# Seven products instead of eight for the gates of two branches, and the first conditioning blocks in half-width loads, in a decoder layer on one core

## The chip, the core and the metric

The kernel runs on one core of a Trainium2 chip. Every time is in microseconds on the device, of one execution; the time of a kernel is the median of its runs. In the profile PE is TensorE (the matmuls), PEld its weight loads, DVE VectorE, ACT ScalarE, POOL GpSimd, SP SyncE; "SPq" marks the instructions that issue transfers.

## The reference, cut to what matters

One layer over 512 prompt tokens and 8 x 4 sample tokens (544 columns), width 1024, in float32. The `gates` are the last 3 x 1024 columns of the combined input projection.

```python
mod = jax.nn.silu(c) @ lp["w_ada"] + lp["b_ada"]
sh1, sc1, g1, sh2, sc2, g2 = [m[:, None, :] for m in jnp.split(mod, 6, axis=-1)]
h = _rmsnorm(x, lp["norm1_g"]) * (1.0 + sc1) + sh1
z = h @ lp["w_in"]
xa, q, k, v, u, gates = jnp.split(z, list(IN_SPLITS), axis=-1)
...
ga, gb, gc = jnp.split(jax.nn.sigmoid(gates), N_BRANCH, axis=-1)
merged = ga * (ya @ lp["w_branch_a"]) + gb * (yb @ lp["w_branch_b"]) + gc * (yc @ lp["w_branch_c"])
x = x + g1 * (merged @ lp["w_out"])
h2 = _rmsnorm(x, lp["norm2_g"]) * (1.0 + sc2) + sh2
a_up, b_up = jnp.split(h2 @ lp["w_ffn_in"], 2, axis=-1)
x = x + g2 * ((jax.nn.silu(a_up) * b_up) @ lp["w_ffn_out"])
```

## The kernel before, in words

Tokens lie along the free dimension: activations are tiles of 128 features x 544 columns, worked in two halves of `H2` = 272. A float32 product is made of three matmuls on a reduced type: each weight tile is split into a rounded part (`whi`, cast on ScalarE) and a rest (`wlo`, VectorE), each activation likewise ("hh" and "hl" for the normed input, 8 tiles each), and a product is hi·hi, lo·hi, hi·lo. So a 128 x 128 weight tile costs 3 matmuls for each half of 272 columns.

All operations are first recorded by the class `Program`, whose `run` puts them in one fixed order per engine with a list scheduler (costs written in the code, priorities by place in the program, `P.high()` puts some first). An engine then works off its order and waits where an operand isn't ready. As one helper issues everything, all rows have line L428; the names of the tiles tell operations apart. Tiles come from pools of fixed size: 56 slots for activations, three raw weight tiles of 1 MiB, four `whi` and four `wlo` tiles of 128 x 512, 4 `aux` and 2 `mm` tiles in PSUM.

The stages in order: (1) the front: x is loaded and turned, the conditioning vector is multiplied with blocks of 512 columns of w_ada (`ada_load`, `ada`: 8 matmuls, a copy to "adae", 4 transposes, a sum on VectorE into "modT"), blocks 2 (scale) and 0 (shift) first, for the first four tiles of the input, blocks 3 and 1 for the other four; `modulate` makes "hf", "hh" and "hl" of a tile. A half block of w_in ("rawx") is loaded for the first main product. (2) The input projection, pooling, attention and the SSM, whose preparation ("vv", "Bb", "Oc") VectorE does beside the products. (3) The three branches: for a pair of output tiles, `gate` multiplies the normed input with the gate's weights (2 x 8 weight tiles, tanh on ScalarE), `mix` multiplies the branch's result with its weights (2 x 4 weight tiles) and merges on VectorE ("tg") and GpSimd; in most pairs a conditioning block is done between. The first branch (b = 0) has its gates computed earlier. (4) w_out, the residual, the second norm, and the FFN, whose `pair` already uses the two-by-two scheme of seven products: sums of weight tiles ("ws") and of activation tiles ("tsum", "th", "tl") on VectorE in place of one product of eight. At the end of the third branch the input is loaded again ("xagain") for the residual.

Of the kernel before, what the change touches and what calls it, by code (L numbers as in the profile page):

```python
# [432 lines left out]
def body(tc, I, O, dbg=None):  # L433
# [4 lines left out]
    with ExitStack() as ctx:  # L438
# [64 lines left out]
        for i, nme in enumerate(("ssm_b_re", "ssm_b_im")):  # L503
            G.dma_start(brow[32 * i:32 * i + 32], I[nme][0].rearrange("g p c -> g (p c)"))
# [10 lines left out]
        up, dp = up, dp  # L515
        ssm = SSM(tc, I, O, locals())
        ssm.load(brow)
# [6 lines left out]

# [51 lines left out]

        def half_u(i, raw):
# [51 lines left out]
        def modulate(k0, scale9, shift9, name):  # L629

            ks = slice(k0, k0 + 4)
            V.tensor_tensor(xs[:, ks], xs[:, ks], scale9[:, ks, 1:9, None].to_broadcast([128, 4, NB, TS]), op=OP.mult)
            V.tensor_tensor(xs[:, ks], xs[:, ks], shift9[:, ks, 1:9, None].to_broadcast([128, 4, NB, TS]), op=OP.add)
            pairs = []
            for k in range(k0, k0 + 4):
# [94 lines left out]
        h1 += modulate(4, sc1, modT[:, 0:8], "h")  # L730
# [355 lines left out]

        yb = [split_a(ybT[t], "yb") for t in range(4)]
        ssm.stage2()
        branch(1, yb, load_b, (4, 5, 8, 9))


# [174 lines left out]
        def product(ps, w, act, start):  # L1266
            for k in range(4):
                (wh, wl), (ah, al) = w[k], act[k]
                with P.unit():
                    for j, (a, b) in enumerate(((wh, ah), (wh, al), (wl, ah))):  # L1270
                        PE.matmul(ps, a, b, start=start and k == 0 and j == 0, stop=k == 3 and j == 2,
                                  skip_group_check=True)

        def pair(i):
# [6 lines left out]
            a0, a1, b0, b1 = a[:, 0:4], a[:, 4:8], b[:, 0:4], b[:, 4:8]  # L1281
            pb, pa_, pd = aux()[:, :H2], mmt()[:, 0, :H2], aux()[:, :H2]
            part, u3, c = st([128, 2, H2], "part"), st([128, 2, H2], "u3"), st([128, N], "ff")
            cl, cr = c[:, t0], c[:, t1]
            product(pb, quarter(a0), X00, True)
            with P.high():
                S.copy(part[:, 0], pb)
            product(pa_, quarter(a1), X10, True)
            with P.high():
                V.tensor_tensor(cl, pa_, part[:, 0], op=OP.add)  # L1290
                S.activation(cl, cl, AF.Silu)
            s1, s2, s3, s4 = (P.tile(up, [128, 4, 128], F32, "ws", "ux", 4) for _ in range(4))
            with P.high():
                V.tensor_tensor(s1, b0, b1, op=OP.add)
                V.tensor_tensor(s2, s1, a0, op=OP.subtract)
            product(pb, quarter(s2), T2, False)
            with P.high():
                S.copy(part[:, 1], pb)
            product(pd, quarter(s1), T1, True)
            with P.high():  # L1300
                V.tensor_tensor(s3, a0, b0, op=OP.subtract)
            product(pb, quarter(s3), T3, False)
            with P.high():
                S.copy(u3[:, 0], pb)
                V.tensor_tensor(u3[:, 0], pd, u3[:, 0], op=OP.add)
            product(pb, quarter(b1), T4, False)
            with P.high():
                V.tensor_tensor(s4, a1, s2, op=OP.subtract)
            product(pd, quarter(s4), X11, False)
            with P.high():  # L1310
                V.tensor_tensor(cr, pd, part[:, 1], op=OP.add)
                V.tensor_tensor(cl, cl, pb, op=OP.mult)
                S.activation(cr, cr, AF.Silu)
            V.tensor_tensor(cr, cr, u3[:, 0], op=OP.mult)
# [4 lines left out]


        t0, t1 = slice(0, H2), slice(H2, N)
        room = P.tile(up, [128, 7, N], F32R, "tsum", "T", 1)
        homes = [room[:, i] for i in range(7)]

        def home(name):
            return homes.pop() if homes else st([128, N], name, F32R)

        T13, T42 = [], []
        for k in range(4):
          with P.high():  # L1330
            ga, gb = gfs[k], gfs[k + 4]
# [472 lines left out]
```

## Time and profile before

| | |
|---|---|
| median of 3 runs | 924.0 us (922.94 to 925.2) |
| the profiled execution: its own time | 922.1 us |
| its span | 920.3 us |
| TensorE busy | 877.9 us, 95% |
| VectorE, ScalarE, GpSimd busy | 571.3, 409.3, 105.4 us |

Durations of matmuls overlap, since they are pipelined: what one costs is read from the distance of starts in an unbroken stretch. A row of the timeline with "x4" stands for 4 in a row of one kind, with the start of the first and the length of all. In a row of the chain likewise. "[1.49 <-ACT hh L428]" is idle time ahead of the instruction and what ended it.

### The profile page before, as it was taken

The numbers are of one execution on the slowest core, as the hardware profiler recorded it, in microseconds if no ns is written. First come the engines' busy times: TensorE is split into PE (matmuls) and PEld (weight loads), VectorE is DVE, ScalarE is ACT, GpSimd is POOL, SyncE is SP. The second block draws the span as 40 slices with busy tenths as digits, with TensorE's granted clock in tenths as the row PEclk, the third lists the DMA queues.
The fourth block names the chain that finished last, engine by engine and source line by source line (L and its number), as shares of the span: only waits on it lengthen the run. The fifth ranks groups of instructions, "written<-read, shape, count | busy, mean of one in ns | idle before, by whom it ended". The sixth has DMA issues, their size and how long they took to land.

```text
span 920.3 us, 17574 instructions
## 1 busy us (share of the span) xinstructions
PE 877.9 (95%) x7064; PEld 822.7 (89%) x7064; DVE 571.3 (62%) x1230; ACT 409.3 (44%) x871; POOL 105.4 (11%) x128
## 2 busy tenths in 40 slices
PE   3899999999989999999999989999999999999996
PEld 1399988998869999999999789999999999999996
DVE  5776778654845223533336798874588874588743
ACT  6464433355553222423344545552255552255554
POOL 4001000254720111012112000000000000000020
PEclk9999999999999999999999999999999999999998
DMA  9863423410214665255524533223433223432212
GB/s 294 317 204 85 120 75 84 136 47 24 80 24 129 186 183 171 93 186 180 185 71 130 167 94 92 69 70 92 138 92 92 71 73 92 134 93 64 68 54 97
DMA packets 128078, 107.14 MB, mean 116 GB/s; under 512 B 4058, under 2 KB 110942, under 8 KB 127973
## 3 DMA queue, kind: packets, MB, share of 16 engines
q1 hardware_dynamic: 127357, 105.24, 37.8%
q8 instruction: 55, 0.90, 0.4%
q0 software_dynamic: 544, 0.75, 0.3%
q14 instruction: 26, 0.21, 0.1%
q10 hardware_dynamic: 96, 0.04, 0.0%
HBM read 102.39 MB, written 4.81 MB: 116 GB/s over the span
## 4 chain that ended last, share of the span: by engine, by line
PE 80%; DVE 11%; DMA 3%; ACT 3%; issue 1%; SPq 1%; POOL 0%; DVEq 0%; ACTq 0%
PE mm L428 55%; PE aux L428 26%; DVE wlo L428 3%; DMA rawx<-in_w_in_dram 2%; ACT whi L428 1%; DVE ffl L428 1%; DVE gf L428 1%; DVE Hst L428 1%; DMA xtok<-in_x_prompt_dram 1%; DMA raw<-in_w_ffn_in_dram 1%; DVE vv L428 1%; SPq L428 1%; DVE rm L428 1%; DVE rn L428 0%; DVE sc L428 0%
## 5 line engine op out<-in xcount | busy, mean ns | idle before, releaser
L428 ACT CAST whi<-raw 128x512 fp32r<-128x512 f32 x224 | 137.3, 614 | 242.4 <-PE mm L428 195.1
L428 DVE TENSOR_TENSOR wlo<-raw,whi 128x512 fp32r<-128x512 f32 x224 | 159.3, 713 | 109.4 <-ACT whi L428 108.3
L428 PE MATMUL mm<-hh,whi 128*128 128x272 f32 x608 | 133.7, 301 | 1.5 <-ACT hh L428 1.5
L428 PE MATMUL mm<-hl,whi 128*128 128x272 f32 x608 | 125.8, 288 | 0.4 <-DVE hl L428 0.4
L428 PE MATMUL mm<-hh,wlo 128*128 128x272 f32 x608 | 125.6, 288 | 0.0
L428 PEld LDWEIGHTS mm<-hh,whi 128*128 128x128 f32 x608 | 94.5, 189 | 13.5 <-issue 9.3
L428 PEld LDWEIGHTS mm<-hl,whi 128*128 128x128 f32 x608 | 95.3, 188 | 0.6 <-DVE hl L428 0.6
L428 PEld LDWEIGHTS mm<-hh,wlo 128*128 128x128 f32 x608 | 95.4, 188 | 0.0
L428 ACT CAST whi<-ws 128x512 fp32r<-128x512 f32 x80 | 48.8, 619 | 66.7 <-PE aux L428 51.3
L428 PE MATMUL mm<-ffh,whi 128*128 128x272 f32 x328 | 68.3, 289 | 0.0
L428 PE MATMUL mm<-ffl,whi 128*128 128x272 f32 x328 | 67.8, 288 | 0.0
L428 PE MATMUL mm<-ffh,wlo 128*128 128x272 f32 x328 | 67.8, 288 | 0.0
L428 POOL TENSOR_TENSOR ssq<-ssq,sq 128x544 f32<-128x544 f32 x10 | 13.6, 1361 | 423.2 <-ACT sq L428 423.2
L428 DVE TENSOR_TENSOR wlo<-ws,whi 128x512 fp32r<-128x512 f32 x80 | 54.4, 688 | 8.8 <-ACT whi L428 5.9
L428 DVE SCALAR_TENSOR_TENSOR xback<-mm,modT,xback 128x272 f32<-128x272 f32 (+3 forms) x64 | 28.4, 479 | 50.0 <-PE mm L428 50.0
L428 PE MATMUL aux<-tsum,whi 128*128 128x272 f32 x280 | 59.2, 291 | 0.0
L428 PE MATMUL aux<-tl,whi 128*128 128x272 f32 x200 | 57.7, 288 | 0.0
L428 PE MATMUL aux<-ghi,wlo 128*128 128x272 f32 x160 | 47.5, 297 | 5.0 <-DVE wlo L428 4.8
L428 PEld LDWEIGHTS mm<-ffh,wlo 128*128 128x128 f32 x328 | 51.5, 188 | 0.0
L428 PEld LDWEIGHTS mm<-ffl,whi 128*128 128x128 f32 x328 | 51.5, 188 | 0.0
L428 PEld LDWEIGHTS mm<-ffh,whi 128*128 128x128 f32 x328 | 51.4, 188 | 0.0
L428 PE MATMUL aux<-th,wlo 128*128 128x272 f32 x160 | 46.2, 289 | 0.0
(414 smaller groups left out, 2067.9 us busy)
## 6 DMA issues: line engine op xcount, KB each, us to landing
raw<-in_w_ada_dram SPq DMA_DIRECT2D x23, 1024.0 KB, 6.5
raw<-in_w_ffn_in_dram SPq DMA_DIRECT2D x44, 512.0 KB, 5.2
raw<-in_w_in_dram SPq DMA_DIRECT2D x16, 1024.0 KB, 6.4
raw<-in_w_ffn_out_dram SPq DMA_DIRECT2D x16, 512.0 KB, 3.8
raw<-in_w_out_dram SPq DMA_DIRECT2D x4, 1024.0 KB, 5.6
raw<-in_w_ffn_out_dram SPq DMA_DIRECT2D x8, 384.0 KB, 3.4
xtok<-in_x_prompt_dram SPq DMA_DIRECT2D x8, 256.0 KB, 6.2
T<-gd SPq DMA_DIRECT2D x32, 64.0 KB, 3.0
```

The source lines that it names most:

```text
L428: return p.add(tag, cost, lambda: fn(*a, **k), ins, writes, fset, nbytes, after, lock)
```

## The change

Two edits. The gates of branches two and three (b = 1, 2) are computed by `seven`, which is taken out of the FFN's `pair` and serves both, except for the first pair of branch two (b = 1, m2 = 0), which keeps the plain gates. With a0, a1 the two halves of the first output tile's weights along the input and b0, b1 those of the second, seven products of 4 tiles each give both output tiles; `sums` makes the sums of the normed input once ("xsum", then "th" and "tl" as `XH`), and each pair makes four sums of weights. In the plain pair the two gates were followed by their mixes in turn; now the two gates come first and then both mixes (the scheduler decides the order).

The second edit: blocks 2 and 0 are loaded and done in halves of 256 columns (`ada_half_load`, `ada_half`), whose rows in memory are 1 KB long; the half block of w_in is loaded third, and `modulate` is called for two, two and four tiles. With it two loads of ssm_b move from GpSimd's queue to ScalarE's, and the small vectors' loads move ahead of those of the SSM.

```diff
-            G.dma_start(brow[32 * i:32 * i + 32], I[nme][0].rearrange("g p c -> g (p c)"))
+            S.dma_start(brow[32 * i:32 * i + 32], I[nme][0].rearrange("g p c -> g (p c)"))
...
+        def ada_half_load(blk, h, home):
+            SY.dma_start(home.rearrange("p (k n) -> p k n", k=KT),
+                         I["w_ada"][0, :, 512 * blk + 256 * h:512 * blk + 256 * h + 256].rearrange("(k p) n -> p k n", p=128))
+            return home
+
+        def ada_half(blk, h, raw):
+
+            ps = aux()[:, 0:256]
+            mm = []
+            for k in range(KT):
+                g = k % 4
+                mm.append(PE.matmul(ps[32 * g:32 * g + 32], cT[:, k, :], raw[:, 256 * k:256 * k + 256],
+                          start=k < 4, stop=k >= 4, tile_position=(0, 32 * g)))
+            ev = st([128, 256], "adah")
+            S.copy(ev, ps)
...
-        first = ada_load(2)
-        second = ada_load(0, (raw_tile(), big[:, 0:2048]))
+        first = [(b, 0, ada_half_load(b, 0, raw_tile())) for b in (2, 0)]
         rawA = half_u(0, big[:, 2048:4096])
+        second = [(2, 1, ada_half_load(2, 1, raw_tile())), (0, 1, ada_half_load(0, 1, big[:, 0:2048]))]
...
-        ada(2, first)
-        early = [ada(0, second)]
+        for x in first:
+            early = [ada_half(*x)]
+        h1 = modulate(0, 2, sc1, modT[:, 0:8], "h")
+        for x in second:
+            ada_half(*x)
         third, fourth = ada_load(3), ada_load(1)
         ssm.load2(early)
-        h1 = modulate(0, sc1, modT[:, 0:8], "h")
+        h1 += modulate(2, 2, sc1, modT[:, 0:8], "h")
...
-                for m in (2 * m2, 2 * m2 + 1):
-                    tg = gate(b, m, rg)
-                    if m == 2 * m2 and m2 < len(blks):
-                        ada(blks[m2])
-                    mix(b, m, rb, y, tg)
+                if b == 1 and m2 == 0:
+                    tg, u3 = gate(b, 0, rg), gate(b, 1, rg)
+                else:
+                    tg, pb, u3 = seven(rg[:, 0:4, 0:128], rg[:, 4:8, 0:128], rg[:, 0:4, 128:256], rg[:, 4:8, 128:256], XH,
+                                       AF.Tanh, 0.5, "tg")
+                    with P.high():
+                        S.activation(u3[:, t0], pb, AF.Tanh, scale=0.5)
+                        S.activation(u3[:, t1], u3[:, t1], AF.Tanh, scale=0.5)
+                if m2 < len(blks):
+                    ada(blks[m2])
+                mix(b, 2 * m2, rb, y, tg)
+                mix(b, 2 * m2 + 1, rb, y, u3)
...
+        def sums(full, act):
...
+            for k in range(4):
+              with P.shift(0 if full is None else -10 ** 6):
+                if full is None:
+                    ga, gb = (st([128, N], "xsum") for _ in range(2))
+                    for g, (hi, lo) in ((ga, act[k]), (gb, act[k + 4])):
+                        V.tensor_tensor(g, hi.bitcast(F32), lo.bitcast(F32), op=OP.add)
+                else:
+                    ga, gb = full[k], full[k + 4]
+                V.tensor_tensor(ga[:, t0], ga[:, t1], ga[:, t0], op=OP.subtract)
+                V.tensor_tensor(ga[:, t1], gb[:, t1], ga[:, t1], op=OP.subtract)
+                V.tensor_tensor(gb[:, t1], gb[:, t1], ga[:, t0], op=OP.subtract)
+                V.tensor_tensor(gb[:, t0], gb[:, t0], gb[:, t1], op=OP.subtract)
+                for g, dst in ((ga, T13), (gb, T42)):
+                    hi, lo = home("th"), home("tl")
+                    S.copy(hi, g)
+                    V.tensor_tensor(lo, g, hi.bitcast(F32), op=OP.subtract)
+                    dst.append((hi, lo))
...
+            s1, s2, s3, s4 = (P.tile(up, [128, 4, 128], F32, "ws", "ux", 4) for _ in range(4))
+            with P.high():
+                V.tensor_tensor(s1, b0, b1, op=OP.add)
+                V.tensor_tensor(s2, s1, a0, op=OP.subtract)
+            product(pb, quarter(s2), X["T2"], False)
...
+        XH = sums(None, h1)
         branch(1, yb, load_b, (4, 5, 8, 9))
```

**The first weight loads, on SyncE** ("raw" and "rawx" are weight tiles of 1 MiB, w_ada the conditioning blocks). Before:

```order
L428 DMA raw<-in_w_ada_dram 128x4x512 x3
L428 DMA rawx<-in_w_ada_dram 128x4x512
L428 DMA rawx<-in_w_in_dram 128x4x512
L428 DMA raw<-in_w_ada_dram 128x4x512 x4
L428 DMA raw<-in_w_in_dram 128x4x512
```

With the change:

```order
L428 DMA raw<-in_w_ada_dram 128x8x256 x2
L428 DMA rawx<-in_w_in_dram 128x4x512
L428 DMA raw<-in_w_ada_dram 128x8x256
L428 DMA rawx<-in_w_ada_dram 128x8x256
L428 DMA raw<-in_w_ada_dram 128x4x512 x4
```

The w_in tile moved from fifth to third place, and four loads have 256 columns instead of 512.

**The first "hl" tiles, on VectorE** (the rests of the normed input; "t", "qi", "P", "aden", "Pr", "Bb", "vv" are the SSM's preparation). Before:

```order
L428 TENSOR_TENSOR wlo<-rawx,whi 128x512 x4
L428 TENSOR_TENSOR modT<-modT,vT 128x36
L428 TENSOR_TENSOR vm<-Ps,Bbw 128x512
L428 SCALAR_TENSOR_TENSOR sc_103<-modT,vT 128x36
L428 TENSOR_REDUCE modT<-aux 128x36
L428 TENSOR_TENSOR xs<-xs,sc_103 128x128
L428 TENSOR_TENSOR modT<-modT,vT 128x36
L428 TENSOR_TENSOR vv<-vv,vm 128x512
L428 TENSOR_TENSOR xs<-xs,modT 128x128
L428 TENSOR_SCALAR hf<-aux,sc_103,modT 128x512
L428 TENSOR_TENSOR vv<-Pr,Bb 128x512
L428 TENSOR_TENSOR hl<-hf,hh 128x544 x2
```

With the change, the first two tiles, and some 20 rows further the next two:

```order
L428 TENSOR_TENSOR wlo<-rawx,whi 128x512 x4
L428 TENSOR_TENSOR xs<-xs,modT 128x64
L428 TENSOR_SCALAR hf<-aux,sc_103,modT 128x512
L428 SCALAR_TENSOR_TENSOR ang<-rk,ang 128x320
L428 COPY rho_241<-RHO 64x16
L428 TENSOR_TENSOR hl<-hf,hh 128x544 x2
```

```order
L428 TENSOR_SCALAR hf<-aux,sc_103,modT 128x512
L428 TENSOR_TENSOR aden<-aden,t_223 128x32
L428 TENSOR_TENSOR qi<-qi,t_224 128x32
L428 COPY P_243<-Pi 64x16
L428 RECIPROCAL aden<-aden 128x32
L428 TENSOR_TENSOR hl<-hf,hh 128x544 x2
```

Two tiles now stand ahead of most of the preparation, which stands between them and the next two.

**One pair of the third branch, on VectorE** ("tg" and "u" are the gates, "mgl" the rests of the merged result). Before:

```order
L428 SCALAR_TENSOR_TENSOR tg<-tg,mm 128x544
L428 TENSOR_TENSOR wlo<-raw,whi 128x512
L428 SCALAR_TENSOR_TENSOR mgl<-merged,mgh 128x544
L428 TENSOR_TENSOR wlo<-raw,whi 128x512 x2
L428 SCALAR_TENSOR_TENSOR tg<-tg,mm 128x544
```

With the change:

```order
L428 TENSOR_TENSOR tg<-aux,part 128x272
L428 TENSOR_TENSOR wlo<-raw,whi 128x512
L428 SCALAR_TENSOR_TENSOR tg<-tg,mm 128x544
L428 TENSOR_TENSOR wlo<-ws,whi 128x512
L428 SCALAR_TENSOR_TENSOR u_1080<-u_1080,mm 128x544
L428 TENSOR_TENSOR wlo<-ws,whi 128x512
L428 SCALAR_TENSOR_TENSOR mgl<-merged,mgh 128x544
L428 TENSOR_TENSOR wlo<-ws,whi 128x512
L428 TENSOR_TENSOR tg<-mm,part 128x272
```

Between the merges stand the splits of the weight sums, and the gates' own adds of 272 columns.

## Rows read from the trace of the kernel before

**Rows 1.** The page: busy times, the clock by slices, the chain's shares.

```profile
PE 877.9 (95%) x7064; PEld 822.7 (89%) x7064; DVE 571.3 (62%) x1230; ACT 409.3 (44%) x871; POOL 105.4 (11%) x128
...
PEclk9999999999999999999999999999999999999998
...
PE 80%; DVE 11%; DMA 3%; ACT 3%; issue 1%; SPq 1%; POOL 0%; DVEq 0%; ACTq 0%
PE mm L428 55%; PE aux L428 26%; DVE wlo L428 3%; DMA rawx<-in_w_in_dram 2%; ACT whi L428 1%; DVE ffl L428 1%; DVE gf L428 1%; DVE Hst L428 1%; DMA xtok<-in_x_prompt_dram 1%; DMA raw<-in_w_ffn_in_dram 1%; DVE vv L428 1%; SPq L428 1%; DVE rm L428 1%; DVE rn L428 0%; DVE sc L428 0%
```

**Rows 2.** The chain up to 60 us: start, length, what, how many.

```profile
52.22 7.89 PE mm L428 x63
```

**Rows 3.** Windows: stretch, length, busy time (instructions) of each engine, clock, DMA.

```profile
425.20:443.25 18.05, 18.05 (x147) 18.05 (x146) 6.68 (x10) 5.87 (x11) 3.34 (x2) 1.00 0.37 110
...
571.20:582.30 11.10, 10.79 (x84) 10.57 (x84) 9.54 (x18) 6.50 (x14) 0.00 (x0) 1.00 0.33 92
...
270.00:309.00 39.00, 39.00 (x334) 36.57 (x333) 16.26 (x28) 13.34 (x28) 1.35 (x1) 1.00 0.41 122
...
30.00:40.00 10.00, 6.74 (x50) 4.17 (x49) 10.00 (x21) 7.18 (x16) 0.00 (x0) 1.00 0.64 224
40.00:50.00 10.00, 10.00 (x72) 7.17 (x72) 2.96 (x10) 2.99 (x6) 0.00 (x0) 1.00 0.89 335
```

**Rows 4.** TensorE's waits over the span: total us, times, longest.

```profile
PE aux L428 <- DVE wlo L428: 4.8, 14, 0.5
PE aux L428 <- DVE vv L428: 2.7, 2, 1.3
```

**Rows 5.** The chain up to 60 us, its front part.

```profile
13.69 15.44 DMA rawx<-in_w_in_dram
...
29.80 2.50 DVE wlo L428 x4
```

**Rows 6.** Timeline of TensorE, 35 to 46 us.

```profile
35.54 0.52 PE L428 MATMUL mm<-hh,whi 128*128 128x272 f32 x2 [1.49 <-ACT hh L428]
36.47 0.52 PE L428 MATMUL mm<-hl,whi 128*128 128x272 f32 x2 [0.40 <-DVE hl L428]
...
39.97 1.05 PE L428 MATMUL aux<-raw,cT 128*32 128x512 f32 x2
...
41.53 1.06 PE L428 MATMUL aux<-raw,cT 128*32 128x512 f32 x6
```

**Rows 7.** Timeline of TensorE in one FFN pair.

```profile
571.38 0.40 PE L428 MATMUL aux<-ghi,wlo 128*128 128x272 f32 x1 [0.32 <-DVE wlo L428]
...
582.49 0.39 PE L428 MATMUL aux<-ghi,wlo 128*128 128x272 f32 x1 [0.32 <-DVE wlo L428]
```

**Rows 8.** VectorE's groups, 571.2 to 582.3 us, and (last) 425.2 to 461.3.

```profile
L428 DVE TENSOR_TENSOR wlo<-raw,whi 128x512 fp32r<-128x512 f32 x4 | 2.7, 686 | 0.1
...
L428 DVE TENSOR_TENSOR ffl<-ff,ffh 128x544 fp32r<-128x544 f32 x1 | 0.7, 718 | 0.0
...
L428 DVE TENSOR_TENSOR ff<-aux,part 128x272 f32<-128x272 f32 x1 | 0.4, 436 | 0.0
...
L428 DVE SCALAR_TENSOR_TENSOR tg<-tg,mm 128x544 f32<-128x544 f32 x4 | 2.9, 722 | 7.9 <-PE mm L428 7.9
```

**Rows 9.** Timeline of SyncE, 440 to 470 us.

```profile
451.01 3.43 SPq L428 DMA_DIRECT2D xagain<-in_x_prompt_dram  x7
```

**Rows 10.** Timeline of TensorE, 459 to 468 us.

```profile
461.38 3.45 PE L428 MATMUL aux<-ca,xagain 32*128 32x32 f32 x32
```

**Rows 11.** Transfers, 20 to 27 us (w_ada) and 52 to 54.5 (w_in, 256 columns).

```profile
DMA packets 1355, 2.71 MB, mean 387 GB/s; under 512 B 36, under 2 KB 36, under 8 KB 1354
...
DMA packets 856, 0.87 MB, mean 347 GB/s; under 512 B 8, under 2 KB 856, under 8 KB 856
```

**Rows 12.** Timeline of VectorE, 24 to 42 us.

```profile
29.06 0.68 DVE L428 TENSOR_TENSOR vv<-Pr,Bb 128x512 f32<-128x512 f32 x1
...
38.91 0.73 DVE L428 TENSOR_TENSOR hl<-hf,hh 128x544 fp32r<-128x544 f32 x1
```

More of the change, by code (lines that the diff above doesn't have):

```diff
@@ L523, in body @@
         G.dma_start(vrow[68:76], I["final_norm_g"].rearrange("(a b) -> a b", b=128))
+        up, dp = up, dp
+        ssm = SSM(tc, I, O, locals())
+        ssm.load(brow)
         cT = ct([128, KT, 32], "cT")
@@ L627, in body, with modulate @@
         S.copy(xs, turned_samples())
[L629 to L633, printed above, removed]
+        def modulate(k0, n, scale9, shift9, name):
+            ks = slice(k0, k0 + n)
+            V.tensor_tensor(xs[:, ks], xs[:, ks], scale9[:, ks, 1:9, None].to_broadcast([128, n, NB, TS]), op=OP.mult)
+            V.tensor_tensor(xs[:, ks], xs[:, ks], shift9[:, ks, 1:9, None].to_broadcast([128, n, NB, TS]), op=OP.add)
             pairs = []
-            for k in range(k0, k0 + 4):
+            for k in range(k0, k0 + n):
                 src = turned(k)
@@ new lines, in product, with seven @@
+        def product(ps, w, act, start):
+            for k in range(4):
+                (wh, wl), (ah, al) = w[k], act[k]
+                with P.unit():
+                    for j, (a, b) in enumerate(((wh, ah), (wh, al), (wl, ah))):
+                        PE.matmul(ps, a, b, start=start and k == 0 and j == 0, stop=k == 3 and j == 2,
+                                  skip_group_check=True)
+        def seven(a0, a1, b0, b1, X, func, scale, name):
+            pb, pa_, pd = aux()[:, :H2], mmt()[:, 0, :H2], aux()[:, :H2]
+            part, u3, c = st([128, 2, H2], "part"), st([128, N], "u3"), st([128, N], name)
+            cl, cr, ur = c[:, t0], c[:, t1], u3[:, t1]
+            product(pb, quarter(a0), X["X00"], True)
+            with P.high():
+                S.copy(part[:, 0], pb)
+            product(pa_, quarter(a1), X["X10"], True)
+            with P.high():
+                V.tensor_tensor(cl, pa_, part[:, 0], op=OP.add)
+                S.activation(cl, cl, func, scale=scale)
+            s1, s2, s3, s4 = (P.tile(up, [128, 4, 128], F32, "ws", "ux", 4) for _ in range(4))
+            with P.high():
+                V.tensor_tensor(s1, b0, b1, op=OP.add)
+                V.tensor_tensor(s2, s1, a0, op=OP.subtract)
+            product(pb, quarter(s2), X["T2"], False)
+            with P.high():
+                S.copy(part[:, 1], pb)
+            product(pd, quarter(s1), X["T1"], True)
+            with P.high():
+                V.tensor_tensor(s3, a0, b0, op=OP.subtract)
+            product(pb, quarter(s3), X["T3"], False)
+            with P.high():
+                S.copy(ur, pb)
+                V.tensor_tensor(ur, pd, ur, op=OP.add)
+            product(pb, quarter(b1), X["T4"], False)
+            with P.high():
+                V.tensor_tensor(s4, a1, s2, op=OP.subtract)
+            product(pd, quarter(s4), X["X11"], False)
+            with P.high():
+                V.tensor_tensor(cr, pd, part[:, 1], op=OP.add)
+                S.activation(cr, cr, func, scale=scale)
+            return c, pb, u3
@@ L1264, in plain_pair @@
             return split_a(f, "ff")
[L1266 to L1272, printed above, removed]
         def pair(i):
@@ L1280, in pair @@
                 SY.dma_start(v, w_ff[:, c0:c0 + 128].rearrange("(k p) n -> p k n", p=128))
-            a0, a1, b0, b1 = a[:, 0:4], a[:, 4:8], b[:, 0:4], b[:, 4:8]
-            pb, pa_, pd = aux()[:, :H2], mmt()[:, 0, :H2], aux()[:, :H2]
-            part, u3, c = st([128, 2, H2], "part"), st([128, 2, H2], "u3"), st([128, N], "ff")
+            c, pb, u3 = seven(a[:, 0:4], a[:, 4:8], b[:, 0:4], b[:, 4:8], XG, AF.Silu, 1.0, "ff")
             cl, cr = c[:, t0], c[:, t1]
-            product(pb, quarter(a0), X00, True)
             with P.high():
[L1287 to L1311, printed above, removed]
                 V.tensor_tensor(cl, cl, pb, op=OP.mult)
-                S.activation(cr, cr, AF.Silu)
-            V.tensor_tensor(cr, cr, u3[:, 0], op=OP.mult)
+            V.tensor_tensor(cr, cr, u3[:, t1], op=OP.mult)
             return split_a(c, "ff")
@@ L1318, in body @@
         plain = [plain_pair(i) for i in range(2)]
[L1321 to L1331, printed above, removed]
[L1332 to L1343 removed]
+        XG = sums(gfs, hh)
         for part, FH in enumerate(PARTS):
```

37 lines of the change are left out of this document (21 added, 16 removed).

## The prediction, made before the changed kernel ran

> **What bounds the kernel now.** I read the page first: busy times, the slices, the chain that ended last. TensorE is busy 877.9 of 920.3 us, its granted clock stands at full speed in all slices but the last, and the chain is 80% PE, of which "mm" and "aux" matmuls make 81 points [rows 1]. So a matmul that goes is time that goes, wherever TensorE never waits. The time that each main matmul takes can't be read from its duration (288 ns, since neighbours overlap); it is read from a stretch of the chain: 63 in 7.89 us, 0.1252 us each [rows 2]. The windows say the same of one pair of the third branch: 18.05 us for 144 matmuls, 0.1253 us each, with TensorE busy through the whole of it, VectorE 6.68 us and ScalarE 5.87 [rows 3]. The list of TensorE's waits has none between 287 and 462 us, where branches two and three lie; of the waits behind the front two recur below: for the SSM preparation on VectorE ("vv", 2.7 us) and in the seven-product pairs of the FFN ("wlo", 14 waits, 4.8 us) [rows 4].
>
> At the start it is different. There the chain is a transfer, then VectorE: the first half block of w_in lands at 29.13 us (13.69 + 15.44), ScalarE and VectorE split it, VectorE's four "wlo" end at 32.3, and only then come the operations that end in "hl" [rows 5]. The first main matmul is at 35.54, the first on "hl" at 36.47; from there TensorE has work nearly all the time [rows 6].
>
> **The gates, part by part.** A plain pair of gates is 2 x 8 tiles x 3 products x 2 column halves = 96 matmuls; by seven products it is 7 x 4 x 3 = 84, of the same shape. Seven pairs: 84 fewer, **84 x 0.1253 = 10.5 us**, if TensorE stays fed. The same rewrite exists already in the FFN, so its price is on the trace: one pair takes 11.10 us for 84 matmuls (10.53 by the pace), VectorE busy 9.54 us of it, so 0.57 us are lost [rows 3], in a "wlo" that is late for the second product or the last one [rows 7]. Will the branches lose as much? Their pair carries 48 mix matmuls besides, so it lasts (84 + 48) x 0.1253 = 16.5 us. VectorE has in it 9 "wlo" and 4 weight sums of 0.69, three adds of 0.44, two "tg" of 0.72, and in branch three two "mgl" as long as a "tg" [rows 8]: 13 x 0.69 + 3 x 0.44 + 2 x 0.72 = 11.7, 13.2 with the last. That is 71 to 80% against 86% in the FFN pair, and the order puts most mix matmuls between the sum products, where the FFN pair starves. I take 0.15 us for each pair, **1.0 us** in all; ends nothing and 7 x 0.57 = 4.0 us.
>
> [...]
>
> The activation sums XH are new: eight adds of 544 columns, sixteen differences of 272, eight "tl" of 544, or 16 x 0.72 + 16 x 0.44 = 18.6 us of VectorE, and eight casts on ScalarE. They stand in VectorE's order from about 269 us (time of before) and are first read after the first plain pair's gates, one conditioning block and the mixes, about 309 us. In 270 to 309 VectorE is busy 16.26 of 39.00 us [rows 3]: 22.7 are free, so they fit; each may hold a "wlo" up by its own 0.72 us, and a "wlo" ready before it is needed absorbs that. Cost **0**; if the cover were gone, up to 18.6.
>
> At the end of branch three SyncE issues two loads of w_out and then seven of the input for the residual; the last of these are read right after the branch. Before, they were issued from 451.01 to 454.4, and TensorE turned to them at 461.38 [rows 9, 10]. A pair shorter by 1.5 us, and raw tiles that come free later within it, cut this margin of 7 us; I take **0.5 us**, ends 0 and 1.
>
> **The front.** Blocks 2 and 0 come in halves of 256 columns, and the w_in half block goes third of five instead of fifth. The five loads of 1 MiB end with it at 29.13 before. Their rows in HBM shrink from 2 KB to 1 KB; loads of such rows elsewhere move 347 GB/s against 387 [rows 11], so 1.05 MB takes 3.02 us instead of 2.71, 1.2 us more over four. The last load then lands at 30.3, the fourth at 27.3, w_in at 24.3, **4.8 us earlier**. Whi to wlo as before ends about 27.4, "hf" and "hl" follow, and the first "hl" matmul can start near 29.5 instead of 36.47.
>
> [...]
>
> But not 7 us are won. Half a block makes two of the four first "hl"; the others wait for the last half (30.3), its matmuls, its copy and transpose, its "modT" rows, two "hf", and the SSM preparation that VectorE's and ScalarE's orders now hold between. Laid end to end with the durations of before, they come at 38.5 to 39.4; before, the last was 38.91 to 39.6 [rows 12]. So what TensorE wins is what it may do between 29.5 and 39.3 with two of the tiles: 30 main matmuls and all of block 3. Before it had done that by about 45, but with 2.5 us of block 1 in between, which is still to do after: 24 main matmuls ahead, 24 x 0.1252 = 3.0 us, and the wait for "adae" inside 39.97 to 41.5, about 1 us [rows 6], which a matmul now fills. **Gain 4.0**; lowest 2, if the first tiles come two or three us late, highest 7, if nothing holds the second half up.
>
> Moved onto this ground: VectorE's SSM preparation ends later (its "vv" began at 29.06) [rows 12]. Between 40 and 50 VectorE was busy 2.96 of 10 us [rows 3], which takes in that work; what does not fit shows at the "vv" waits. The ssm_b loads go from POOL's queue to ScalarE's and vrow's transpose to before 20 us: neither ends a chain, 0.
>
> **Sum.** The profiled execution took 922.1 us, 1.8 more than its span of 920.3 (the same afterwards, I take it). 922.1 - 10.5 + 1.0 + 0.5 - 4.0 = 909.1. The median of the runs is 1.9 above that execution, so **911.0**. Bounds: 84 matmuls with no stall, front 7: 924.0 - 10.5 - 7 = 906.5; stalls 4.0, residual 1, front 2: 924.0 - 10.5 + 5.0 - 2 = 916.5. Change within 0.2% (1.85 us) can't be told from none here.
>
> **Rivals.** *B, the front gives nothing.* The last "hl" is as late as before, and VectorE's postponed preparation runs into the "vv" waits, which are VectorE's already. For it: VectorE is full from 30 to 40 (10.00) [rows 3]. Against: 7 us free in the next ten. 911.0 + 4.0 = **915.0**. *C, the pairs lose as in the FFN*, 0.57 each: for it, 13 operations of 0.69 in a row when weights of a pair land together; against, the mixes that fill. 911.0 + 3.0 = **914.0**; with B 918.0. *D, slower than before*: the sums XH, issued into one in-order VectorE queue ahead of "wlo" that TensorE reads, are exposed. All of it gives 911.0 + 18.6 = **929.6**; it decides from 13 us exposed, 70% of it. Against: 22.7 us free there, and whi and wlo have four buffers each. *E, the change doesn't do what it says*: pairs last as long as before because something other than the count of matmuls sets them, 911.0 + 9.5 = **920.5**, or no change at all with B, 924.5. Against: TensorE has no idle in a pair, and the weight loads fall with the matmuls.
>
> **Chances.** Forecast 0.62 (own range 906.5 to 913.5), B 0.20, C 0.11 with or without B, D 0.04, E 0.03. From 905 to 918 takes in all of the first three but tails, and leaves some 0.15 out. Faster by over 0.2%: the first three and the half of E that ends at 920.5, 0.94; same 0.02; slower D, 0.04.
>
> **What would show it.** In the profile after: mm and aux matmuls of 272 columns 84 fewer; a pair of branch three 16.5 to 16.7 us long, with TensorE's idle under 0.2 in each; no wait for "xsum", "tl" or "wlo" between 265 and 310; w_in landing near 24.3 and the last half at 30.3; the first main matmul near 28.5 and the last of the first four "hl" at 38.5 to 39.5; TensorE at 60 us some 4 us ahead in matmuls done. It is wrong if TensorE waits over 0.5 us in each pair, if "vv" waits grow by more than 2 us, or if the first "hl" matmul is after 33.

## The result, and the profile after

The changed kernel takes 913.2 us (median of 4 runs, 912.69 to 914.04) against 924.1 before (4 runs): ratio 0.9882, interval 0.9867 to 0.9897, or 10.9 us less, where the sum of the forecast had 13.1. A later set of 5 runs gave 913.98 and 0.9902 (0.9884 to 0.9920).

The page answers to [rows 1] with busy times and the chain's shares:

```profile
PE 870.1 (95%) x7012; PEld 815.3 (89%) x7012; DVE 633.4 (69%) x1339; ACT 435.4 (48%) x936; POOL 107.3 (12%) x126
...
PE 81%; DVE 10%; DMA 4%; ACT 3%; issue 1%; SPq 0%; DVEq 0%; ACTq 0%
```

VectorE has 62 us more to do, TensorE 8 us less, and TensorE is as much the chain as before. The trace has 5676 matmuls of 272 columns where before has 5760: the 84. Two pairs of the third branch in the windows (columns as in [rows 3]); the first has an idle of 0.2 us ahead of a product, the other none:

```profile
415.06:432.09 17.03, 16.85 (x135) 16.64 (x133) 13.95 (x23) 8.95 (x19) 3.35 (x2) 1.00 0.29 94
432.09:448.63 16.54, 16.54 (x134) 16.48 (x132) 10.90 (x16) 8.91 (x19) 3.54 (x2) 1.00 0.65 213
```

The plain pair took 18.05. To see where the rest went I cut each span at three events that all kernels have: the last merge of the first branch on VectorE, the first transpose of the input read back on TensorE, and the first reciprocal of the second norm on VectorE. The differences between them, in us, for this kernel and those of the experiments (one profiled execution each):

| kernel | up to the last merge | branches two and three | read-back, w_out | rest |
|---|---|---|---|---|
| before | 288.2 | 173.2 | 49.5 | 409.4 |
| changed | 285.4 | 163.3 | 53.1 | 410.4 |
| changed, again | 286.0 | 163.1 | 52.8 | 410.3 |
| gates only | 290.2 | 165.6 | 51.5 | 408.8 |
| halves only | 286.1 | 173.2 | 49.4 | 409.2 |
| read-back first | 285.4 | 165.7 | 49.7 | 410.3 |
| read-back first, again | 285.1 | 166.4 | 49.7 | 410.0 |
| first tiles ahead | 286.0 | 166.3 | 51.4 | 410.9 |
| second half on VectorE | 284.8 | 163.0 | 51.4 | 410.8 |
| combo | 285.7 | 163.0 | 49.6 | 410.8 |
| combo, again | 283.9 | 163.0 | 49.6 | 409.5 |
| filler | 284.7 | 162.8 | 49.6 | 412.2 |
| sums more | 285.6 | 165.0 | 51.1 | 409.9 |
| eight pairs | 293.6 | 169.0 | 51.2 | 410.4 |

So from before to changed: the front won 2.8, the branches 9.9, the read-back lost 3.6 of it, and the rest 1.1 (by unrounded times), which makes the 8.0 us between the two spans. (The medians are 10.9 apart, because before's profiled execution, 922.1 us, was faster than the four that give its median, and the changed kernel's, 914.0, the slowest of its four.)

TensorE's waits show the read-back as a new line; the others have changed little against [rows 4]:

```profile
PE aux L428 <- DVE wlo L428: 4.9, 14, 0.5
...
PE mm L428 <- ACT hh L428: 2.5, 1, 2.5
PE aux L428 <- DVE vv L428: 2.3, 3, 1.4
PE aux L428 <- POOL sc L428: 2.3, 3, 1.8
...
PE aux L428 <- DMA xagain<-in_x_prompt_dram: 1.7, 2, 1.4
```

And three windows of 4 us, with the granted clock (the share of its full speed that TensorE was given) as the third column from the end. It is at 1.00 nearly everywhere, but not in the first and the last of these:

```profile
32.00:36.00 4.00, 4.00 (x28) 2.64 (x27) 1.88 (x11) 3.91 (x8) 0.00 (x0) 0.57 1.04 382
256.00:260.00 4.00, 3.62 (x26) 2.12 (x24) 2.17 (x7) 3.45 (x13) 2.82 (x3) 1.00 0.00 0
452.00:456.00 4.00, 3.66 (x21) 3.52 (x19) 0.86 (x2) 2.59 (x5) 0.00 (x0) 0.57 0.71 243
```

0.57 over 4 us is a stretch mostly at 0.50, the granted clock from 32.5 to 35.5 us and from 452.5 to 455.5: 0.43 x 4 = 1.7 us of matmul work lost in each, an estimate from the granted share. Ahead of the first TensorE had waited 2.5 us for the first tile of the normed input, ahead of the last 1.4 us for the read-back. Before's profiled execution had its clock at 1.00 in both places, from 28 to 44 us and from 448 to 464. Its mean granted clock, 0.997, is at the top of what 38 later runs of before show, 0.992 to 0.997; the nine runs of the changed kernel show 0.991 to 0.993.

The read-back on TensorE, which answers to [rows 10], and what SyncE issued, to [rows 9]:

```profile
448.72 1.04 PE L428 MATMUL aux<-ca,xagain 32*128 32x32 f32 x10
451.16 0.98 PE L428 MATMUL aux<-ca,xagain 128*128 128x128 f32 x7 [1.40 <-DMA xagain<-in_x_prompt_dram]
452.49 1.75 PE L428 MATMUL aux<-ca,xagain 128*128 128x128 f32 x7 [0.34 <-DMA xagain<-in_x_prompt_dram]
```

```profile
424.16 13.40 SPq L428 DMA_DIRECT2D raw<-in_w_out_dram  x2
437.62 1.03 SPq L428 DMA_DIRECT2D xagain<-in_x_sample_dram  x2
438.69 1.37 SPq L428 DMA_DIRECT2D xagain<-in_x_prompt_dram  x3
441.13 0.38 SPq L428 DMA_DIRECT2D raw<-in_w_out_dram  x1
441.61 3.07 SPq L428 DMA_DIRECT2D xagain<-in_x_prompt_dram  x5
```

The second load of w_out stands in the queue until a raw tile is free (13.40 us for two issues, 12.6 of them a wait for VectorE's "wlo"), and a third comes between the loads of the input; the last of them are issued up to 444.7 and TensorE turns to them at 448.7: 4 us, where before had 7. The load of w_out between them, issued at 441.13, lands at 449.8, 1 us after TensorE has turned to the input.

### The profile page after: what moved, and what is told of

Read it like the earlier page. It is cut to its first block, busy times and chain, and to the rows that moved or that the text cites. A ratio compares the mean times of both kernels' runs of the same rounds, so it can differ in the third digit from the quotient of the medians.

```text
span 912.3 us, 17678 instructions
## 1 busy us (share of the span) xinstructions
PE 870.1 (95%) x7012; PEld 815.3 (89%) x7012; DVE 633.4 (69%) x1339; ACT 435.4 (48%) x936; POOL 107.3 (12%) x126
## 4 chain that ended last, share of the span: by engine, by line
PE 81%; DVE 10%; DMA 4%; ACT 3%; issue 1%; SPq 0%; DVEq 0%; ACTq 0%
PE mm L428 47%; PE aux L428 34%; DVE wlo L428 3%; ACT whi L428 2%; DVE ffl L428 1%; DMA raw<-in_w_ada_dram 1%; DVE gf L428 1%; DMA xagain<-in_x_prompt_dram 1%; DMA raw<-in_w_ffn_in_dram 1%; DMA xtok<-in_x_prompt_dram 1%; DVE Hst L428 1%; DVE sc L428 0%; DVE vv L428 0%; DVE rm L428 0%; DVE ws L428 0%
## 5 line engine op out<-in xcount | busy, mean ns | idle before, releaser
L428 ACT CAST whi<-raw 128x512 fp32r<-128x512 f32 (+1 forms) x217 | 132.4, 614 | 179.4 <-PE mm L428 125.3
L428 DVE TENSOR_TENSOR wlo<-raw,whi 128x512 fp32r<-128x512 f32 (+1 forms) x217 | 152.9, 710 | 71.6 <-ACT whi L428 69.8
L428 PE MATMUL mm<-hh,whi 128*128 128x272 f32 x412 | 95.1, 306 | 2.5 <-ACT hh L428 2.5
L428 PE MATMUL mm<-hl,whi 128*128 128x272 f32 x412 | 87.7, 289 | 0.3 <-DVE hl L428 0.3
L428 PE MATMUL mm<-hh,wlo 128*128 128x272 f32 x412 | 87.7, 289 | 0.0
L428 PEld LDWEIGHTS mm<-hl,whi 128*128 128x128 f32 x412 | 65.8, 189 | 0.6 <-DVE hl L428 0.6
L428 PEld LDWEIGHTS mm<-hh,wlo 128*128 128x128 f32 x412 | 65.6, 189 | 0.0
L428 DVE SCALAR_TENSOR_TENSOR xback<-mm,modT,xback 128x272 f32<-128x272 f32 (+3 forms) x64 | 28.5, 479 | 50.5 <-PE mm L428 50.4
L428 PE MATMUL aux<-tsum,wlo 128*128 128x272 f32 x216 | 62.0, 287 | 0.0
L428 PE MATMUL aux<-th,whi 128*128 128x272 f32 x216 | 62.0, 287 | 0.0
L428 PEld LDWEIGHTS aux<-tsum,whi 128*128 128x128 f32 x378 | 60.7, 188 | 0.9 <-ACT u L428 0.4
```

Source lines behind the costliest of these rows:

```text
L428: return p.add(tag, cost, lambda: fn(*a, **k), ins, writes, fset, nbytes, after, lock)
```

## The experiments

Each was timed in 5 rounds beside the kernel before on the same chip; the ratios are to that kernel.

**Gates only.** The front of before, the gates of the change (the diff is that of the change without its first part).

```diff
+        XH = sums(None, h1)
```

> The gates alone, on the front of before. Theory: 84 matmuls fewer are worth 10.5 us in the branches, TensorE doesn't wait within a pair (0.2 us in all after), and some 3 us go again where the input is read back for the residual (1.7 us of waits and as much by the halved clock behind them): 924.1 - 10.5 + 3.4 = 917.0, ratio 0.992. First rival (the pairs lose 0.57 each as in the FFN): 924.1 - 6.5 + 3.4 = 921. Second rival (the read-back stall belongs to the earlier front and not to the gates): no stall here, 913.6.

917.33 us, ratio 0.9932 (0.9918 to 0.9945): the theory's time, though not by its terms. The branches shortened by 7.6 us in this profile (table). The read-back has 1.3 us of waits, so it belongs to the gates, but no fall of the clock behind them (1.00 from 448 to 460): its stretch is 2.0 us longer than before's, not 3.4. The 7.6 instead of 9.9 go with a stall of TensorE, which comes back below.

**Halves only.** The front of the change, the plain gates of before.

> The half blocks alone, with the plain gates. Theory: the front is worth the 2.3 to 2.8 us by which the changed kernel is ahead at 60 and at 285 us, so 921.5, ratio 0.997; the clock falls to half in the same 32 to 36 us after the wait for the first tile. Rival (the front is worth the predicted 4.0, and what is missing came from the gates): 920.1. Second rival (what the front wins is lost again in the SSM part): 924.

919.78 us, ratio 0.9957 (0.9945 to 0.9970), 3.8 us less: the theory's 921.5 was wrong and the first rival's 920.1 right, with the forecast 4.0 for the front and not the 2.8 that the changed kernel's profile showed. The clock fell here too (granted 0.90 and 0.67 in the windows of 4 us from 28 to 36). The profile of gates only shows where the difference can come from: it has before's front, and here the clock fell between 36 and 44 us (granted 0.73 and 0.84 in windows of 4 us), which it hadn't in before's profile. Up to 60 us, TensorE has done 110 matmuls of 272 columns in gates only, 124 in before, 142 in the changed kernel and 143 in halves only. Between two fronts that both have a fall of the clock, 32 matmuls, 32 x 0.125 = 4.0 us, are the gain; against a before without one it is 18, 2.3 us. Such counts scatter: in the other five profiles with the changed kernel's front they are 137 to 148, 1.4 us from end to end. The time of halves only is the firmer measure.

**Read-back first.** The loads of the input ahead of three loads of w_out:

```diff
-            rw = load_w(I["w_out"][0, :, 256 * m2:256 * m2 + 256], KT, 256)
+            rw = load_w(I["w_out"][0, :, 256 * m2:256 * m2 + 256], KT, 256, xload if m2 else ())
```

> The changed kernel with the ten loads that bring the input back issued ahead of the second, third and fourth load of w_out. Theory: the two loads of w_out in front of them in SyncE's queue (1 MiB each, the first of them blocked until a raw tile is free) make the transposes wait 1.7 us, and the idle lowers TensorE's clock for another 1.7 us of loss: both go, 913.2 - 3.3 = 909.9, ratio to before 0.9847, granted clock 1.00 in that stretch. Rival (the loads wait for free slots, which the sums XH hold, not for the loads of w_out): they are issued no earlier, 913.2, ratio 0.988. Second rival (the later loads of w_out make the products of w_out wait instead): 913 to 915, with waits on raw there.

910.5 us, ratio 0.9868 (0.9851 to 0.9886). SyncE's and TensorE's timelines:

```profile
429.92 7.91 SPq L428 DMA_DIRECT2D xagain<-in_x_prompt_dram  x8
439.63 13.57 SPq L428 DMA_DIRECT2D raw<-in_w_out_dram  x3
```

```profile
451.17 3.45 PE L428 MATMUL aux<-ca,xagain 32*128 32x32 f32 x32
```

All ten are issued by 437.8, TensorE doesn't wait, and the stretch up to the norm is 49.7 us, as long as before's 49.5. Of the rivals, slots hold nothing up, and the later loads of w_out cost nothing. The time is 2.7 and not 3.3 us below the changed kernel's, which is from another set of runs, while the branches were 2.4 us longer in the profile. For that I ran it again beside the changed kernel itself:

> The changed kernel itself once more, as the partner of the next on one chip: 913.2, ratio 0.988. Which of the three places shows the halved clock (32, 256, 452 us) is left to chance by the theory; the wait for the input's second loads is there again, 1 to 1.7 us.

> The kernel with the input's second loads ahead of the loads of w_out, once more. Theory: no wait at the read-back, so 1.1 to 1.7 us less than its partner always, and 1.7 more where the clock fell there: 910.5, ratio 0.986. Rival (what it won was chance of the clock): the same as its partner within 1 us.

913.98 (0.9902) and 910.01 us, ratio 0.9854 (0.9834 to 0.9874): 4.0 us less than its partner. The partner shows waits of 1.2 us at the read-back and a granted clock of 0.58 in the window from 452 to 456; the kernel with the read-back first has neither (1.00 in that window). That the order of the loads makes the waits is shown. Their size is less sure. Seven profiles have the wait (1.1 to 1.7 us): in five the clock stays up behind it (1.00 from 448 to 460) and the read-back stretch is 51.1 to 51.5 us, 1.6 to 2.0 more than before's; in the two of the changed kernel it falls, and they are 3.3 and 3.6 more. By time the edit is worth 2.7 and 4.0 us here and 1.2 between the two kernels with the second half on VectorE (below). And the nine runs of read-back first have a granted clock of 0.992 to 0.993, no higher than the changed kernel's, so that a gain by the clock isn't shown over their runs.

**The stall in the branches.** In four profiles (gates only, read-back first twice, first tiles ahead) the branches take 165.6 to 166.4 us, and TensorE's waits have 1.2 to 1.5 us for "part"; in six with the new gates they take about 163. (Sums more and eight pairs are taken up below.) In read-back first TensorE waits in one pair like this, with the line of ScalarE that goes ahead of it:

```profile
328.96 0.52 PE L428 MATMUL aux<-tsum,whi 128*128 128x272 f32 x2 [0.65 <-ACT part L428]
329.93 0.39 PE L428 MATMUL aux<-tsum,wlo 128*128 128x272 f32 x1 [0.44 <-DVE wlo L428]
...
333.90 0.52 PE L428 MATMUL aux<-tsum,whi 128*128 128x272 f32 x2 [0.70 <-ACT part L428]
```

```profile
323.18 1.14 ACT L428 CAST whi<-raw 128x512 fp32r<-128x512 f32 x2 [3.14 <-DMA raw<-in_w_in_dram]
```

In the changed kernel the same cast comes at 320.67, after a wait of 0.62. The load behind it was issued at the same time in both, and landed 8.6 us after its issue in read-back first, 6.1 us after it in the changed kernel:

```profile
314.51 0.37 SPq L428 DMA_DIRECT2D raw<-in_w_in_dram  x1
```

```profile
314.52 0.37 SPq L428 DMA_DIRECT2D raw<-in_w_in_dram  x1
```

So the weights of a pair land with no reserve, and 2.5 us of delay in the transfer, with the same issue, make a pair lose 1.8 us in waits; the branches are 2.3 to 3.1 us longer, the rest not located. The windows of read-back first and of the changed kernel (DMA share and GB/s last) show something of the transfer:

```profile
325.00:327.00 2.00, 2.00 (x18) 2.00 (x17) 2.00 (x6) 0.03 (x1) 0.60 (x1) 1.00 0.06 25
```

```profile
325.00:327.00 2.00, 2.00 (x18) 2.00 (x17) 2.00 (x3) 0.92 (x3) 0.74 (x2) 1.00 0.04 8
```

In read-back first (both profiles) and first tiles ahead the traffic ends with some 2 us at a share of 0.06 and 24 to 25 GB/s, a sixteenth (in gates only, where the next pair stalls, with 1 us); and from 321 us in read-back first the last rows of 1 KB of the late load trickle in, 7 to 20 a us, beside those of the next one: as if one of the 16 DMA engines were behind, an estimate from the share of 0.06 alone. Why stays open; it wasn't tried.

**First tiles ahead.** The operations of the first two tiles before the four "wlo" on VectorE:

```diff
-        h1 = modulate(0, 2, sc1, modT[:, 0:8], "h")
+        with P.high():
+            h1 = modulate(0, 2, sc1, modT[:, 0:8], "h")
```

> The changed kernel with the operations that make the first two tiles of the normed input put ahead of the four wlo of the first weights. Theory (the 2.5 us for which TensorE waits for the first tile cost its clock, and with it 1.7 us more): the first main matmul comes near 28, the clock stays at 1.00 between 32 and 36, and TensorE is 1.5 to 3 us further at 60 us: 913.2 - 2.0 = 911.2, ratio 0.986. Rival (the second half of the tiles at 39.6 bounds the front; with two tiles of PSUM only 24 main matmuls can be done before it): TensorE waits behind them instead, 913.2, ratio 0.988.

915.73 us, ratio 0.9903 (0.9887 to 0.9920): no gain. The start of TensorE's work:

```profile
28.93 0.52 PE L428 MATMUL mm<-hh,whi 128*128 128x272 f32 x2 [0.86 <-ACT hh L428]
...
36.25 0.44 PE L428 MATMUL aux<-ca,adah 128*128 128x128 f32 x2 [1.36 <-ACT adah L428]
...
39.44 0.52 PE L428 MATMUL mm<-hh,whi 128*128 128x272 f32 x2 [0.24 <-ACT hh L428]
```

Everything the theory asked for came: the first tile 1.4 us earlier than in the changed kernel (30.37), the clock at 1.00 from 32 to 36. But 24 main matmuls are done at 34.7, and then TensorE waits for the second half; at 60 us it has done 143 matmuls, 142 without the edit. The rival holds: the second half bounds the front. (The profiled run, at 916.28 the slowest of five from 912.44 on, also has the stall in the branches, so the time says little about the front.) (That two tiles in PSUM are why no more than 24 can be done is read from the code, not tried.)

**Second half on VectorE.** With the edit above, the second halves' copies go from ScalarE, where they stood behind a table load (1.28 us, at 33.69 in the changed kernel), to VectorE, and the next two tiles are put first too:

```diff
-            S.copy(ev, ps)
+            with P.high():
+                (V.tensor_copy if h else S.copy)(ev, ps)
```

> The changed kernel with the first two tiles ahead of the wlo, and the second halves of blocks 2 and 0 copied out by VectorE instead of ScalarE, with the next two tiles put first as well. Theory (the front is bounded by the second half, behind ScalarE's table load and copies): the last two hl of the first four start near 37.5 instead of 39.6, and at 60 us TensorE is some 1.5 to 2 us (12 to 16 matmuls) further than with the first tiles ahead alone, 143: 911.5, ratio 0.986. Rival (something later, the next conditioning block or the weights, takes over as the bound): 143 matmuls at 60 us, 913.2.

911.83 us, ratio 0.9878 (0.9862 to 0.9894); 153 matmuls at 60 us, 10 more, and the clock stays up in the front (1.00 from 28 to 44). The last two "hl" of the first four start at 38.27, not at 37.5, but ahead of the 39.53 of first tiles ahead. The three other profiles with this front (combo twice, filler) have 148 to 155 matmuls at 60 us, against 137 to 148 in the seven with the changed kernel's front: on average 7 more, 0.9 us, so part of the theory's 1.5 to 2. The time, 1.4 us under the changed kernel, lies within the intervals of both.

> The same with the input's second loads ahead of the loads of w_out. Theory (the two are independent, one at 40 us, one at 450): 910.5 - 1.7 = 908.8, ratio to before 0.984. Rival (the front gives nothing by itself): 910.5, ratio 0.9868.

910.67 us, ratio 0.9862 (0.9847 to 0.9876): no clear gain over read-back first alone, with 148 matmuls at 60 us, and 1.2 us under second half on VectorE, timed beside it. The rival's 910.5 is nearer than the theory's 908.8, but the two can't be told apart here.

**Sums more.** Each of the eight sums of "hh" and "hl" made twice.

```diff
+                        for _ in range(2):
-                            V.tensor_tensor(g, hi.bitcast(F32), lo.bitcast(F32), op=OP.add)
+                                V.tensor_tensor(g, hi.bitcast(F32), lo.bitcast(F32), op=OP.add)
```

> The changed kernel with each of the eight sums of hh and hl made twice, 8 x 0.72 = 5.8 us more on VectorE ahead of the branches. Theory (the sums lie in VectorE's free time and end at 297, some 9 us before the first product that reads them): they now end near 303, TensorE has no wait for them, 913.2, ratio to before 0.988. Rival (the sums are on the path, as in the forecast's case D): 913.2 + 5.8 = 919.0, ratio 0.995.

914.84 us, ratio 0.9904 (0.9891 to 0.9918). The rival's 919 is out. The sums end at 312.1 instead of the changed kernel's 297.1 (15 us for 5.8 of work), after the first product that reads them; the last rest on VectorE and that product on TensorE:

```profile
311.38 0.72 DVE L428 TENSOR_TENSOR tl<-xsum,th 128x544 fp32r<-128x544 f32 x1
```

```profile
309.56 0.41 PE L428 MATMUL aux<-tsum,whi 128*128 128x272 f32 x2
```

Still TensorE has no wait for a sum, since it reads them tile by tile. The cover takes in most of the 5.8 us, perhaps all: my 303 was wrong, the branches are 1.7 us longer than in the changed kernel's profile (0.4 of it a wait for "adae", the rest not located), and the median is 1.6 us above the changed kernel's first set of runs, but only 0.9 above the second, within the intervals.

**Eight pairs.** The plain pair made in seven products as well:

```diff
-                if b == 1 and m2 == 0:
+                if False:
```

> The changed kernel with the first pair of branch two in seven products too: 12 matmuls fewer, 1.5 us, but the sums are read from about 288 us instead of 306. Theory (18.6 us of sums need the first plain pair as cover): they can't end before about 297, so TensorE waits several us there, 913.2 - 1.5 + 5 = 916.7, with waits on tl, th or tsum. Rival (the scheduler puts the sums earlier and other products between): no wait, 911.7, ratio 0.986.

927.72 us, ratio 1.0042 (1.0028 to 1.0056): 12 matmuls fewer make it 14.5 us longer than the changed kernel. The waits for "th" and "tl" are only 2.0 us:

```profile
300.69 0.39 PE L428 MATMUL aux<-th,whi 128*128 128x272 f32 x1 [1.41 <-ACT th L428]
301.64 0.40 PE L428 MATMUL aux<-tl,whi 128*128 128x272 f32 x1 [0.55 <-DVE tl L428]
```

The larger part lies ahead of the branches: 8.2 us more up to the last merge. It isn't the sums XH, which VectorE does from 275.6 on, as far ahead of the last merge as in the changed kernel. VectorE's order is that of the changed kernel up to 245 us; then the scheduler has put the four weight sums of the new pair into the attention, where VectorE waits for their load ahead of the softmax and of "yal" (an operand of the first branch's mixes), and TensorE waits for "yal":

```profile
245.16 1.29 DVE L428 TENSOR_TENSOR ws<-raw 128x512 f32<-128x512 f32 x2 [1.25 <-DMA raw<-in_w_in_dram]
```

```profile
247.53 0.39 PE L428 MATMUL mm<-yal,whi 128*128 128x272 f32 x1 [1.58 <-DVE yal L428]
```

The waits for "sc" grow to 3.8 us (2.3 in the changed kernel), and the clock is at 0.50 to 0.65 for 12 us:

```profile
248.00:252.00 4.00, 2.89 (x11) 2.38 (x11) 3.76 (x9) 2.79 (x10) 0.91 (x1) 0.57 0.00 0
252.00:256.00 4.00, 3.57 (x14) 1.95 (x15) 3.54 (x12) 2.81 (x10) 2.43 (x3) 0.50 0.52 130
256.00:260.00 4.00, 3.72 (x19) 2.22 (x15) 1.26 (x5) 2.72 (x10) 0.69 (x2) 0.65 0.02 5
```

Between 245 and 269 us TensorE loses 9.0 us on the changed kernel. That the weight sums start it is read from the order and the waits, not tried. In the branches themselves 5.7 us are lost, with 2.0 us of waits for the sums, 1.1 for a conditioning load and a granted clock of 0.84 from 304 to 312. The direction was the theory's, the place and the size were not. Of case D of the prediction, the sums XH exposed, it shows these 2.0 us of waits.

**Filler.** Combo again, and combo with 14 transposes read by nobody ahead of a wait of 1.8 us in the attention.

```diff
+                    if (tp, n, h) == (1, 2, 0):
+                        for _ in range(14):
+                            PE.transpose(pt[:, 0:128], ident, ident)
```

> The kernel of combo once more, as the partner of the next one on the same chip: 910.7, ratio 0.986, with the clock at half behind the wait of 1.8 us for sc in the attention (near 256 us), as in both profiles of kernels with this front.

> Combo with 14 transposes of the identity, read by nobody, put on TensorE ahead of the transposes of sc for which it waits 1.8 us in the attention. Theory (the wait itself is 1.8 us, but the clock that falls behind it costs as much again): the fillers (some 0.13 us each) fill the wait, the clock stays at 1.00 from 252 to 260, and a kernel with more work takes 1.7 us less, ratio to before 0.984. Rival (the clock near 256 follows something else, or the fillers push the transposes back): the same time as its partner or up to 1 us more.

Combo takes 910.43 us, ratio 0.9858 (0.9836 to 0.9880), runs from 907.73 to 913.79; filler 910.89, ratio 0.9861 (0.9844 to 0.9878), runs from 910.37 to 910.98. In combo's first profile, the wait and the two windows behind it:

```profile
254.69 0.69 PE L428 MATMUL aux<-ca,sc 128*128 128x128 f32 x2 [1.80 <-POOL sc L428]
```

```profile
252.00:256.00 4.00, 2.20 (x13) 1.21 (x12) 3.60 (x11) 3.75 (x14) 2.26 (x3) 0.81 0.22 49
256.00:260.00 4.00, 4.00 (x25) 2.33 (x22) 1.64 (x6) 2.78 (x9) 2.08 (x2) 0.76 0.00 0
```

With the filler:

```profile
252.72 1.69 PE L428 MATMUL aux<-ca 128*128 128x128 f32 x14
254.68 0.44 PE L428 MATMUL aux<-ca,sc 128*128 128x128 f32 x2 [0.27 <-POOL sc L428]
```

```profile
252.00:256.00 4.00, 3.73 (x30) 2.63 (x28) 3.60 (x11) 3.75 (x14) 2.25 (x3) 1.00 0.22 46
256.00:260.00 4.00, 3.62 (x32) 2.42 (x34) 1.73 (x6) 3.12 (x12) 2.07 (x2) 1.00 0.00 0
```

The fillers fit the wait and the clock stays at 1.00. But combo's second profile, without fillers, has 1.00 there too and the shortest span of all (905.9): behind this wait the clock falls in one execution and not in the next. The expectation of 1.7 us failed. The granted clock of filler's runs, 0.995 to 0.998, is even a little above combo's, 0.994 to 0.997, so the clock alone doesn't set the median. Filler's profile loses 2.7 us to combo's second in the rest of the kernel (412.2 against 409.5); 1.1 of it is the wait for "ghi" told below, and whether the fillers have a part in it isn't shown. The spread was 0.6 us instead of 6, over few runs.

The best versions, read-back first (910.0 to 910.5), combo (910.4 to 910.7) and filler (910.9), beat the kernel before by some 13 us and can't be told from one another; beside the changed kernel itself only read-back first was timed.

## Why the prediction was right, and where it was off

The time came 2.2 us later than the forecast 911.0, on its side and within its range. That it is only 2.2 is in part luck. For an execution like the profiled one the sum gave 909.1, and the changed kernel's profiled execution took 914.0: 4.9 later. The forecast put the median 1.9 above that execution, as in before, whose profiled execution had an unusually high clock; it came 0.8 below.

- **84 matmuls at 0.1253.** Right. The branches went from 173.2 to 163.3, 9.9 us or 0.118 us for each of the 84, where the term and its stalls gave 9.5; where nothing stalls, 10.4 (filler).
- **Stalls in the pairs, 1.0.** In the changed kernel 0.2 us of waits. The pair of 16.5 to 16.7 came as 16.54 and 17.03. But rival C is not dead: when a pair's weights land late, the branches lose 2.3 to 3.1 us, from another cause than C named, a transfer and not VectorE's load.
- **The sums XH, 0.** Right, and of 5.8 us more 1.7 at most showed. Read too early, as in eight pairs, they cost 2.0 us of waits.
- **The read-back, 0.5 with ends 0 and 1.** This step failed. The place was right and the direction too, but it cost 3.6 us in the changed kernel's profile, and 1.6 to 2.0 in five others with the same wait: the margin of 7 us before shrank to 4, which gave waits of 1.1 to 1.7 us, and in the changed kernel's two profiles a fall of the clock behind them (0.57 and 0.58 from 452 to 456). I had taken the margin from the time of issue and not counted the 1 MiB transfers of w_out in the same stretch. A fall of the clock behind a wait, here and in the front, is in no term of the sum.
- **The front, 4.0.** Right by the time of halves only (3.8 us) and by counts between fronts in the same state of the clock (4.0), and 2.8 in the one pair of profiles that the sum was made for. The steps were off: the first main matmul came at 30.37 and not 28.5, the first on "hl" at 31.22 and not 29.5. The transfer wasn't late. From 23 us on all but one of the packets are rows of under 2 KB, so w_in is in by then, ahead of the forecast 24.3; but its cast begins only at 25.28, with no idle of ScalarE before it, and the four "wlo", behind other work of VectorE, run from 26.71 to 29.2 where the forecast ended them at 27.4. The transfers from 23 to 27 us in the changed kernel and in before, and the cast:

```profile
DMA packets 1377, 1.39 MB, mean 348 GB/s; under 512 B 17, under 2 KB 1376, under 8 KB 1377
```

```profile
DMA packets 775, 1.55 MB, mean 387 GB/s; under 512 B 20, under 2 KB 20, under 8 KB 775
```

```profile
25.28 2.17 ACT L428 CAST whi<-rawx 128x512 fp32r<-128x512 f32 x4
```

That lateness cost nothing that shows, as first tiles ahead has it. The last two "hl" came at 39.63 to 40.9, forecast 38.5 to 39.5. TensorE was 2.3 us ahead at 60 us, not some 4, against a before whose clock had not fallen (1.00 from 28 to 44).
- **VectorE's postponed SSM work.** Rival B is out: the waits for "vv" went from 2.7 to 2.3 us.
- **The rest of the kernel.** 1.1 us longer in the profile, not foreseen; 408.8 to 412.2 over all kernels, whose code there hardly differs. The trace places it: in the second norm ScalarE waits 1.64 us for a load of FFN weights, 0.18 in before, and behind it TensorE 1.3 us for "ghi", 0.3 in before. The lines of the changed kernel and of before:

```profile
517.11 1.14 ACT L428 CAST whi<-raw 128x512 fp32r<-128x512 f32 x2 [1.64 <-DMA raw<-in_w_ffn_in_dram]
```

```profile
524.73 1.14 ACT L428 CAST whi<-raw 128x512 fp32r<-128x512 f32 x2 [0.18 <-DMA raw<-in_w_ffn_in_dram]
```

The load is issued at the same time after the norm's first reciprocal (6.7 us) and lands at 15.3 instead of 13.8. Ten of the twelve profiles with new gates have the long wait, gates only and combo's second not, nor has either kernel with the old ones. The reason stays open.

The price of the rows of 1 KB was right: 348 GB/s against 387 in the two lines above, as the forecast took it from elsewhere in the kernel. The last of these rows moves at 29.1 us all the same, not at 30.3.

## What to carry to other kernels

In this kernel the gain in matmuls was paid out only as far as the transfers that follow it kept up (of 9.9 us won in the branches, 3.6 went at the read-back): after shortening a stage, go through the queue for the loads whose margin was set by the old length, and subtract the transfers that stand ahead of them, not only the issue. The extra input that the seven products need, 18.6 us of VectorE by the forecast's estimate, was free here under the plain pair that covers it (no wait for a sum), and one step more can move other work too: with the eighth pair the sums gave 2.0 us of waits, while the new pair's weight sums, put ahead of the attention's work and waiting there for their load, went with a loss of 9. Look at each engine's order after every such edit. And before a difference of 2 us is explained, look whether the granted clock in the two profiles agrees: here one window of 4 us at 0.57 is 1.7 us.

## What I had not expected of the hardware

- After the same wait of TensorE the granted clock fell in one execution and not in the next: behind the 1.8 us for "sc", windows of 4 us show 1.00 in five profiles (before, changed twice, combo's second, the second of read-back first) and 0.57 to 0.76 in seven. A window at 0.57 is 1.7 us of matmul work lost, by the estimate above.
- In the changed kernel's front it wasn't chance. All seven profiles with the changed kernel's front have a fall between 28 and 36 us, where TensorE waits 1.7 to 2.7 us for the first tile (1.7 us of matmul work lost in five of them, 3.3 and 3.4 in changed again and the second of read-back first); none of the five with the first tiles ahead has one, where the longest waits are 0.7 to 1.4 us. The time didn't follow: first tiles ahead gained nothing by it, since the second half bounds the front.
- A transfer of 1 MiB with the same time of issue (314.5) was first used 2.5 us later in one execution than in another, and the late one's traffic ended at a share of 0.06, 25 GB/s.
